# A decoder trunk's MLP on one Trainium2 core: the first matrix by seven half-size products in place of eight

## The chip, the cores and the metric

The kernel runs on one core of a Trainium2 chip. The metric is the device time of one execution in microseconds; the median of several runs is compared. The program is one straight list of instructions for each engine: PE (TensorE, with PEld for its weight loads), DVE (VectorE), ACT (ScalarE), POOL (GpSimd), SP (SyncE, which here issues the weight transfers). An engine works through its list in order, and an instruction waits until semaphores tell it that its inputs are there and its output's buffer is free.

## The reference, cut to what matters

One layer of a decoder for 512 prompt tokens and 8 sample tokens (520 columns in all), width 1024. Token mixing (an RWKV-7 branch beside an RG-LRU branch), cross-attention, and a squared-ReLU MLP of hidden width 4096 follow one another, each with a residual and a layer norm behind it. The edit touches the MLP:

```
D_MODEL = 1024;  D_FF = 4 * D_MODEL;  ALPHA = (2 * DEPTH) ** 0.25
x = LN2(ALPHA * x + cross_attention(x))
h = relu(x @ mlp_up) ** 2          # (520, 1024) @ (1024, 4096)
x = LN3(ALPHA * x + h @ mlp_down)  # (520, 4096) @ (4096, 1024)
```

## The kernel before, in words

Activations lie with features on the 128 partitions and tokens along the free side: `ff0` is x behind the second norm (128 x 8 x 520, eight blocks of 128 features), `q` (also called `z3`) the MLP's sum. Every large product is computed in a number format of the PE that keeps fewer bits than float32, with each operand cut in two: a high part (a copy that rounds) and a low part (what the copy lost). `mm3` then issues three matmuls for each 128 x 128 weight block and each half of the tokens: high weights by high x, high weights by low x, low weights by high x. `Y` is the pair of high and low part of the MLP's input (tiles `hl2`, `hl3`).

`split_w` brings a weight block: a transfer of 512 KB on SP's queue into a raw tile `wr` (three buffers), ACT's copy to the high part `wh` (L95), DVE's subtraction for the low part `wl` (L98).

The MLP runs in NF = 8 groups f of 512 hidden features. A group has four *up units* (`u_up`, 128 hidden columns each, all 8 blocks of K: 8 x 3 x 2 = 48 matmuls of about 260 columns) and, one group later, four *down units* (`u_down`, 256 output columns each as two blocks of K = 512: 2 x 4 x 3 x 2 = 48 matmuls). Behind an up unit come ACT's Relu out of PSUM (L1575), DVE's product max(p,0)*r (L1576), ACT's rounding copy into `hd`, the group's hidden tile (L1577), and DVE's low part of it (L1578). Behind a block of a down unit DVE adds the PSUM result into `q` (L1593, and L1591 for f = 0). `hd` is one of two tiles of the earlier x, called `xH` and `xL` in the rows by turns.

Two helpers order the work. `adv` runs whole units in the order of the list `units`, with the weights of two more units prepared ahead. `halves` runs units by halves of the tokens (`HA` columns first, the rest second), so that the first units of the MLP start while the second norm still works on the other half, and the last four down units finish the first half while the output norm `ln_out` begins. The order in which an engine's instructions stand is set by the program's order and a scheduler behind it, which moves instructions of different units past each other. PSUM has two tiles `mm` of two halves, two tiles `ps`, and one each `ch0` and `ch1`.

Of the kernel before, what the change touches and what calls it, by code (L numbers as in the profile page):

```python
# [36 lines left out]
def build(tc, d, dbg=None):  # L37
# [111 lines left out]
    def unit(src, fn, shape=(KT, 128), extra=0):  # L149
        units.append([src, fn, shape, extra, None])  # L150
# [712 lines left out]
    def slot(t, i, n=1):  # L863
        return t[:, 64 * i:64 * (i + n)].rearrange("p (j b) -> p j b", b=NB)
# [421 lines left out]
    state["x"] = [wx, None]  # L1286
    B1 = ExitStack()
    kv = {}
    at = B1.enter_context(tc.tile_pool(name="at", bufs=2, reuse_waits="tile"))

    def u_rw(i):
        def run(w, half=None):
# [63 lines left out]
    def ln_stats(z, t0, n, wide=False):  # L1356
        if wide:
            p = mmps()
            pp = [p[:, 0], p[:, 1]]
        else:  # L1360
            pp = [ps4(), ps4()]
        st = at.tile([128, 2, 6], F32, tag="bst", name="bst")
# [4 lines left out]
        mv = at.tile([128, 4], F32, tag="mv", name="mv")  # L1367
# [25 lines left out]

    def ln_samples(z):

        zc = at.tile([128, KT, NB], F32, tag="zc", name="zc", bufs=1)
# [16 lines left out]
        t = at.tile([64, 128], F32, tag="sxn", name="sxn", bufs=1)  # L1413
# [155 lines left out]
    def u_up(f, i):  # L1569
        def run(w, half=None):  # L1570
            hd = X[f % 2]
            r = LR.tile([128, T], F32, tag="ya" if i % 2 else "yb", name="r")

            def epi(v, p):
                ACT.activation(v(r), p, AF.Relu)  # L1575
                DVE.scalar_tensor_tensor(v(r), p, 0.0, v(r), op0=OP.max, op1=OP.mult)  # L1576
                ACT.copy(v(hd[:, i, :]), v(r))  # L1577
                DVE.tensor_tensor(v(hd[:, 4 + i, :]), v(r), v(hd[:, i, :].bitcast(F32)), op=OP.subtract)  # L1578
            prod(w, Y, half, epi)
        wunit("mlp_up", f * 512 + i * 128, run, {1: 1, 2: 2, 3: 2}.get(4 * f + i, 0))  # L1580

    def u_down(f, i):
        def run(w, half=None):
            hd = X[f % 2]
            for a in range(2):
                j = 2 * i + a

                def epi(v, p):
                    z = v(z3[:, j, :])
                    if f == 0:  # L1590
                        DVE.scalar_tensor_tensor(z, v(ff0[:, j, :]), ALPHA, p, op0=OP.mult, op1=OP.add)  # L1591
                    else:
                        DVE.tensor_tensor(z, z, p, op=OP.add)  # L1593
                prod(w, (hd[:, 0:4], hd[:, 4:8]), half, epi, [(k, k) for k in range(4)],
                     slice(a * 128, (a + 1) * 128))
        unit(d["mlp_down"][0][f * 512:(f + 1) * 512, i * 256:(i + 1) * 256].rearrange("(k p) n -> p k n", p=128),
             run, (4, 256), int(f == NF - 1 and i == 3))
# [11 lines left out]
    for f in range(NF + 1):
        for i in range(4):  # L1610
            if f < NF:
                u_up(f, i)
        for i in range(4):
            if f > 0:
                u_down(f - 1, i)
# [32 lines left out]
    for h in range(XH):  # L1648
# [10 lines left out]
        if h > 1:  # L1659
# [18 lines left out]
    for n in ("ln3_g", "ln3_b"):  # L1678
# [66 lines left out]
```

## Time and profile before

| | us |
|---|---|
| runs of the kernel before | 1388.75, 1395.51, 1400.05 (median 1395.51) |
| the profiled execution | 1402.65 |
| span of its instructions | 1400.9 |
| PE busy in the span | 1319.4 (94%) |
| DVE busy | 897.1 (64%) |
| ACT busy | 592.1 (42%) |
| POOL busy | 249.7 (18%) |

The profiled execution was 7.1 us above the median of the runs, and within 2.6 us of the slowest. The MLP takes the stretch from about 1006 us (its first half unit) to about 1377 us (the last matmul of its last down unit); the second norm overlaps its begin and the output norm its end.

### The profile page before, as it was taken

How to read it: one execution, taken by the hardware profiler on the slowest of the kernel's cores; microseconds unless marked ns; L12 is line 12 of the kernel's file. 1: busy time of each engine (PE TensorE's matmuls, PEld its weight loads, DVE VectorE, ACT ScalarE, POOL GpSimd, SP SyncE). 2: the span in 40 equal slices, each digit the busy share in tenths (PEclk: the TensorE clock that was granted, in tenths of full speed). 3: DMA queues.
4: the chain of work that ended last, by engine and by line, in shares of the span. 5: the costliest groups of instructions: out<-in, count | busy, mean ns of one | idle time of the engine just before them, and what ended most of it. 6: DMA issues, size and time to landing. Idle time of an engine off the chain costs nothing. (4 is left out here: it accounts for less than half of the span.)

```text
span 1400.9 us, 27360 instructions
## 1 busy us (share of the span) xinstructions
PE 1319.4 (94%) x11242; PEld 1225.5 (87%) x11242; DVE 897.1 (64%) x1742; ACT 592.1 (42%) x1069; POOL 249.7 (18%) x327
## 2 busy tenths in 40 slices
PE   7998999999999998889999999989899999999996
PEld 7997988798878886788879999768899999999996
DVE  5578877796679675887855554756754444444455
ACT  4484375536643665442254334432442332233221
POOL 6311001200020012325423133351110000000002
PEclk9999999998999798898999999999999999999998
DMA  7422412222222032474559545683222233323311
GB/s 197 137 72 63 128 54 63 90 76 65 68 79 84 21 93 91 131 209 138 169 155 288 160 133 176 208 289 121 76 83 86 91 93 92 94 90 97 96 61 62
DMA packets 205971, 160.28 MB, mean 114 GB/s; under 512 B 12430, under 2 KB 190912, under 8 KB 205335
## 3 DMA queue, kind: packets, MB, share of 16 engines
q1 hardware_dynamic: 182502, 104.36, 25.5%
q0 software_dynamic: 14592, 47.80, 10.1%
q10 hardware_dynamic: 8752, 6.39, 1.4%
q8 instruction: 88, 1.44, 0.5%
q14 instruction: 37, 0.30, 0.1%
HBM read 137.11 MB, written 21.40 MB: 113 GB/s over the span
## 5 line engine op out<-in xcount | busy, mean ns | idle before, releaser
L47 PE MATMUL mm<-xH,wh 128*128 128x260 f32 (+2 forms) x1824 | 481.3, 293 | 5.4 <-ACT wh L95 2.2
L47 PE MATMUL mm<-xL,wh 128*128 128x256 f32 (+2 forms) x1824 | 477.2, 290 | 1.3 <-DVE ff L1593 1.0
L47 PE MATMUL mm<-xH,wl 128*128 128x264 f32 (+2 forms) x1568 | 454.8, 290 | 0.8 <-DVE wl L98 0.8
L47 PEld LDWEIGHTS mm<-xH,wh 128*128 128x128 f32 x1824 | 330.9, 191 | 17.0 <-issue 4.3
L95 ACT CAST wh<-wr 128x1024 fp32r<-128x1024 f32 x178 | 185.9, 1050 | 369.9 <-PE mm L47 309.7
L47 PEld LDWEIGHTS mm<-xL,wh 128*128 128x128 f32 x1824 | 330.8, 191 | 9.5 <-issue 5.1
L98 DVE TENSOR_TENSOR wl<-wr,wh 128x1024 fp32r<-128x1024 f32 x178 | 224.0, 1262 | 143.2 <-ACT wh L95 142.5
L47 PEld LDWEIGHTS mm<-xH,wl 128*128 128x128 f32 x1568 | 299.8, 191 | 7.6 <-issue 4.3
L47 PE MATMUL mm<-hl,wh 128*128 128x260 f32 (+2 forms) x1536 | 283.8, 286 | 2.2 <-DVE r L1576 1.4
L47 PEld LDWEIGHTS mm<-hl,wh 128*128 128x128 f32 x1536 | 239.2, 190 | 3.9 <-DVE r L1576 1.6
L47 PE MATMUL mm<-hl,wl 128*128 128x260 f32 (+2 forms) x768 | 219.3, 286 | 0.0
L47 PEld LDWEIGHTS mm<-hl,wl 128*128 128x128 f32 x768 | 145.8, 190 | 0.6 <-issue 0.5
L1593 DVE TENSOR_TENSOR ff<-ff,mm 128x520 f32<-128x520 f32 (+2 forms) x64 | 40.1, 627 | 74.1 <-PE mm L47 73.6
L47 PE MATMUL mm<-xL,wl 128*128 128x260 f32 (+2 forms) x256 | 72.6, 284 | 0.0
L1700 POOL TENSOR_TENSOR xn<-xn,ln_g 128x512 f32<-128x512 f32 x3 | 3.8, 1276 | 355.4 <-ACT xn L1699 355.4
L47 PEld LDWEIGHTS mm<-xL,wl 128*128 128x128 f32 x256 | 48.2, 188 | 0.0
L720 DVE TENSOR_TENSOR Tm<-Tm,tmp 64x30 f32<-64x30 f32 (+14 forms) x120 | 40.5, 337 | 3.4
L47 PE MATMUL mm<-mh,wh 128*128 128x256 f32 x128 | 38.4, 301 | 3.9 <-ACT ft L1129 1.8
L718 DVE TENSOR_TENSOR tmp<-Am,Tm 64x30 f32<-64x30 f32 (+14 forms) x120 | 39.5, 329 | 3.2
L47 PE MATMUL mm<-mh,wl 128*128 128x256 f32 x128 | 37.8, 296 | 3.6 <-DVE wl L98 3.6
L794 DVE SCALAR_TENSOR_TENSOR Sbd<-Sbd,DL,ch 64x64 f32<-64x64 f32 x112 | 31.4, 280 | 15.2 <-PE ch L47 12.4
L533 POOL COPY OUTC<-ut 128x3 f32<-128x3 f32 x8 | 2.9, 366 | 203.0 <-ACT ut L529 203.0
(475 smaller groups left out, 2014.4 us busy)
## 6 DMA issues: line engine op xcount, KB each, us to landing
wr<-in_w_in_dram SPq DMA_DIRECT2D x58, 512.0 KB, 4.4
wr<-in_mlp_up_dram SPq DMA_DIRECT2D x32, 512.0 KB, 4.1
wr<-in_mlp_down_dram SPq DMA_DIRECT2D x32, 512.0 KB, 3.6
vc<-in_cache_mem_v_dram POOLq DMA_DIRECT2D x32, 256.0 KB, 7.3
ff<-in_cache_mem_k_dram POOLq DMA_DIRECT2D x32, 256.0 KB, 4.0
gat_d<-gt POOLq DMA_DIRECT2D x16, 260.0 KB, 2.6
wr<-in_xa_wk_dram SPq DMA_DIRECT2D x8, 512.0 KB, 5.4
wr<-in_xa_wv_dram SPq DMA_DIRECT2D x8, 512.0 KB, 4.9
```

The lines of the kernel that those rows point to most:

```text
L47: r = nc.tensor.matmul(*a, **k)
L95: a = ACT.copy(h, raw)
L98: DVE.tensor_tensor(l, raw, h.bitcast(F32), op=OP.subtract)
L533: POOL.tensor_copy(COUT[:, 0, :, i], ut[:, S:S + 3])
L718: DVE.tensor_tensor(tv, Am[:, i + 1:32, i:i + 1].to_broadcast([64, n, i]), Tm[:, i:i + 1, 0:i].to_broadcast([64, n, i]), op=OP.mult)
L720: DVE.tensor_tensor(Tm[:, i + 1:32, 0:i], Tm[:, i + 1:32, 0:i], tv, op=OP.add)
L794: DVE.scalar_tensor_tensor(Sn[s][hs, hs], So[s][hs, hs], Q[s]["DL"][hs, c - 1:c], PX[hs, cs], op0=OP.mult, op1=OP.add)
L1593: DVE.tensor_tensor(z, z, p, op=OP.add)
L1700: POOL.tensor_tensor(t[0:n], t[0:n], gb[0][0:n, hs], op=OP.mult)
```

## The change

Thirteen pairs of up units, from (1,1) to (7,1) in the changed kernel's naming (group, pair in the group), are no longer computed as 2 x 48 matmuls each. The 1024 x 256 weights of a pair are seen as 2 x 2 blocks (K halves by columns), the 520 tokens as two halves of 260, and the 2 x 2 product is formed from seven half-size products in place of eight (Winograd's form of Strassen's scheme). One product is K = 512, 128 columns, 260 tokens: 4 x 3 = 12 matmuls, so a pair takes 84.

- Four sums of weight blocks (`s1` to `s4`, 128 x 512 each) are formed by POOL for each pair; all seven weight operands are cut into high and low part by ACT and DVE in pieces of 128 x 512 (L1626, L1627), as are the down units' blocks. The cuts run eight blocks ahead (`LEAD`) in a ring of ten slots, and the raw weights have five buffers.
- Four sums of the input (`y_sums`) are formed once, by DVE and POOL, and cut into `TH` and `TL`, each in two pieces of 128 x 520.
- The seven results are combined out of PSUM by ACT (the copy `p1`, L1678) and DVE (seven additions of 128 x 260, L1681 to L1701). Each of the four finished quarters is squared by DVE (L1672), rounded by ACT (L1673), and its low part is formed by POOL (L1674).
- The order of units: six up units (f = 0 and two of f = 1) by halves as before; then the four down units of f = 0; then pair (1,1); then for f = 2 to 7 and each of its two pairs the pair and two down units of f - 1; the last four down units by halves. The input's sums stand beside those first six up units and four down units.
- The norms' small tiles get a pool of their own (`lnp`), the attention's pool `at` goes to the other side of memory and closes earlier, which leaves room for `TH` and `TL`. The third norm's gains and offsets are loaded before the last two down units of f = 6 and no longer before the MLP's full units.

```
     for i in range(6):
         u_up(i // 4, i % 4)
     rest = [u_down(0, i) for i in range(4)] + [u_pair(1, 1)]
     for f in range(2, NF):
         for ip in range(2):
             rest += [u_pair(f, ip), u_down(f - 1, 2 * ip), u_down(f - 1, 2 * ip + 1)]
     last = [u_down(NF - 1, i) for i in range(4)]
...
+    def need(n):
+        while cut[0] < min(n, len(blocks), cap[0]):
+            li, key = blocks[cut[0]]
+            load_to(li + 1)
+            h, l = slot(cut[0])
+            src = got[li][key]
+            ACT.copy(h, src)                                              # L1626
+            DVE.tensor_tensor(l, src, h.bitcast(F32), op=OP.subtract)     # L1627
+            cut[0] += 1
...
+    def mm3b(out, n, x, xk, sl, first=True, last=True):
+        need(n + 1 + LEAD)
+        mm3(out, slot(n), x, [(k, xk + k) for k in range(4)], sl, first, last)
...
+            POOL.tensor_tensor(s1, a21, a22, op=OP.add)                   # L1652
+            POOL.tensor_tensor(s2, s1, a11, op=OP.subtract)
+            POOL.tensor_tensor(s3, a11, a21, op=OP.subtract)
+            POOL.tensor_tensor(s4, a12, s2, op=OP.subtract)               # L1655
...
+            ya, yb = (LR.tile([128, T], F32, tag=tg, name="r").rearrange("p (h n) -> p h n", h=2) for tg in ("ya", "yb"))
+            p1, u2, w5, r = ya[:, 0], ya[:, 1], yb[:, 0], yb[:, 1]
+            def out(v, i, sl):
+                h, l = hd[:, 2 * ip + i, sl], hd[:, 4 + 2 * ip + i, sl]
+                DVE.scalar_tensor_tensor(v, v, 0.0, v, op0=OP.max, op1=OP.mult)   # L1672
+                ACT.copy(h, v)                                                    # L1673
+                POOL.tensor_tensor(l, v, h.bitcast(F32), op=OP.subtract)          # L1674
+            a = t[:, 0, TT]
+            mm3b(a, n0_, Y, 0, T0)
+            ACT.copy(p1, a)                                               # L1678
+            a = t[:, 1, TT]
+            mm3b(a, n0_ + 1, YT[1], 0, TT)
+            DVE.tensor_tensor(u2, a, p1, op=OP.add)                       # L1681
+            a = psc(npair[0] % 2)[:, TT]
+            mm3b(a, n0_ + 2, YT[0], 0, TT)
+            DVE.tensor_tensor(w5, a, u2, op=OP.add)
+            t = mmps()
+            a = t[:, 0, TT]
+            mm3b(a, n0_ + 3, Y, 4, T0)
+            DVE.tensor_tensor(r, a, p1, op=OP.add)                        # L1688
+            out(r, 0, T0)
...
+    def y_sums(z):
...
+        for (lo, hi), a, b in zip(ks, ra, rb):
+            DVE.tensor_tensor(a, z[:, lo, T1], z[:, lo, T0], op=OP.subtract)      # L1722
+            POOL.tensor_tensor(b, z[:, hi, T1], a, op=OP.subtract)                # L1723
...
```

Three places show how the engines' lists change. The first is DVE's list where the MLP's first half units end, from the product of half unit (5,0) (the sixth unit's first half) to that of (3,1). `r` is the square's tile, `xH`/`xL` the hidden tile's low part, `ts` a sum of the input, `TL` its low part, `wl` the low part of weights. Before:

```order
L1576 SCALAR_TENSOR_TENSOR r<-mm,r 128x256
L1578 TENSOR_TENSOR xL<-r,xL 128x256
L1576 SCALAR_TENSOR_TENSOR r<-mm,r 128x264
L1578 TENSOR_TENSOR xH<-r,xH 128x264
L1576 SCALAR_TENSOR_TENSOR r<-mm,r 128x264
L1578 TENSOR_TENSOR xL<-r,xL 128x264
L1576 SCALAR_TENSOR_TENSOR r<-mm,r 128x264
L1578 TENSOR_TENSOR xL<-r,xL 128x264
L98 TENSOR_TENSOR wl<-wr,wh 128x1024
L1576 SCALAR_TENSOR_TENSOR r<-mm,r 128x264
```

In the changed kernel the same stretch of DVE's list, from the product of (0,1) on, reads (twelve rows, which reach only to that of (2,1)):

```order
L1577 SCALAR_TENSOR_TENSOR r<-mm,r 128x264
L1627 TENSOR_TENSOR wl<-wr,wh 128x512 x2
L1579 TENSOR_TENSOR xH<-r,xH 128x264
L1719 TENSOR_TENSOR TL<-ts,TH 128x520
L1577 SCALAR_TENSOR_TENSOR r<-mm,r 128x264
L1719 TENSOR_TENSOR TL<-ts,TH 128x520
L1627 TENSOR_TENSOR wl<-wr,wh 128x512
L1579 TENSOR_TENSOR xH<-r,xH 128x264
L1627 TENSOR_TENSOR wl<-wr,wh 128x512
L1719 TENSOR_TENSOR TL<-ts,TH 128x520
L1577 SCALAR_TENSOR_TENSOR r<-mm,r 128x264
L1627 TENSOR_TENSOR wl<-wr,wh 128x512
```

Between the products of two half units, where one low part stood alone, there are now three to five more instructions: pieces of the input's sums and half blocks of weights.

The second place is POOL's list. Before, POOL had nothing between the second norm's last low part and the output norm. In the changed kernel stand there, around pair (1,1), the sums for pair (2,1), the four low parts of pair (1,1), the four of pair (2,0), and the sums for pair (3,0):

```order
L1652 TENSOR_TENSOR ws<-wr 128x512
L1654 TENSOR_TENSOR ws<-wr 128x512
L1653 TENSOR_TENSOR ws<-ws,wr 128x512
L1655 TENSOR_TENSOR ws<-wr,ws 128x512
L1674 TENSOR_TENSOR xL<-r,xL 128x260 x4
L1674 TENSOR_TENSOR xH<-r,xH 128x260 x4
L1652 TENSOR_TENSOR ws<-wr 128x512
L1654 TENSOR_TENSOR ws<-wr 128x512
L1653 TENSOR_TENSOR ws<-ws,wr 128x512
L1655 TENSOR_TENSOR ws<-wr,ws 128x512
L1674 TENSOR_TENSOR xH<-r,xH 128x260 x4
```

The sums of a pair that comes later stand ahead of the low parts of the pair that is running; pairs (1,1) and (2,0) have no down unit between them.

The third place is DVE's list in the steady stretch, one pair's seven results with the cuts between them (`ps`, `ch`, `mm` are PSUM tiles, `ws` a weight sum). In the changed kernel:

```order
L1681 TENSOR_TENSOR r<-mm,r 128x260
L1684 TENSOR_TENSOR r<-ch,r 128x260
L1627 TENSOR_TENSOR wl<-wr,wh 128x512
L1627 TENSOR_TENSOR wl<-ws,wh 128x512
L1688 TENSOR_TENSOR r<-mm,r 128x260
L1627 TENSOR_TENSOR wl<-ws,wh 128x512
L1672 SCALAR_TENSOR_TENSOR r<-r 128x260
L1692 TENSOR_TENSOR r<-ps,r 128x260
L1693 TENSOR_TENSOR r<-ps,r 128x260
L1672 SCALAR_TENSOR_TENSOR r<-r 128x260
L1627 TENSOR_TENSOR wl<-wr,wh 128x512
L1697 TENSOR_TENSOR r<-mm,r 128x260
```

Before, two up units had there:

```order
L1576 SCALAR_TENSOR_TENSOR r<-mm,r 128x520
L1578 TENSOR_TENSOR xH<-r,xH 128x520
L98 TENSOR_TENSOR wl<-wr,wh 128x1024
L1576 SCALAR_TENSOR_TENSOR r<-mm,r 128x520
L1578 TENSOR_TENSOR xH<-r,xH 128x520
L98 TENSOR_TENSOR wl<-wr,wh 128x1024
```

Four long instructions for the two units' results became eleven short ones that each wait for one of the seven products or for the one ahead, and the weights are cut in smaller pieces between them.

More of the change, by code (lines that the diff above doesn't have):

```diff
@@ L1361, in ln_stats @@
             pp = [ps4(), ps4()]
[L1362 removed]
+        st = lnp.tile([128, 2, 6], F32, tag="bst", name="bst")
         for h in range(2):
@@ L1580, in u_up, with slot @@
         wunit("mlp_up", f * 512 + i * 128, run, {1: 1, 2: 2, 3: 2}.get(4 * f + i, 0))
-    def u_down(f, i):
-        def run(w, half=None):
+    LEAD = 8
+    ring, loads, got, blocks = [], [], [], []
+    cut, cap = [0], [8]
+    def slot(n):
+        if n // 2 == len(ring) < 5:
+            p = (wsp, wx, state["x"][1], wsp, wsp)[n // 2]
+            ring.append((p.tile([128, KT, 128], F32R, tag="wh", name="wh"),
+                         p.tile([128, KT, 128], F32R, tag="wl", name="wl")))
+        t, k = ring[n // 2 % 5], n % 2 * 4
+        return t[0][:, k:k + 4], t[1][:, k:k + 4]
@@ new lines, in build, with raw_tile, more_raws @@
+    spare = []
+    def raw_tile(src, shape):
+        raws.append(raws.pop(0))
+        raw = raws[-1]
+        if raw in spare:
+            if shape[0] == 4:
+                raw = raw.rearrange("p (k a) n -> p k (a n)", a=2)
+        else:
+            raw = raw.tile([128, *shape], F32, tag="wr", name="wr")
+        SP.dma_start(out=raw, in_=src)
+        return raw
+    def more_raws():
+        for tg in ("wh", "wl"):
+            spare.append(state["x"][1].tile([128, KT, 128], F32, tag=tg, name="wr"))
+        raws.extend(spare)
@@ new lines, in load_to @@
+    def load_to(n):
+        while len(got) < min(n, len(loads)):
+            got.append(loads[len(got)]())
+    def need(n):
[7 more added lines that the diff above has]
+            cut[0] += 1
+            if cut[0] < len(blocks) and blocks[cut[0]][0] > li:
+                got[li] = None
+                load_to(li + 4 if cap[0] > 8 else min(li + 4, 4))
@@ new lines, in build, with cut_ @@
+    YT = []
+    def y_sums(z):
+        TH = tp.tile([128, 4, 4, HT], F32R, name="TH")
+        TL = tp.tile([128, 4, 4, HT], F32R, name="TL")
+        YT[:] = [(TH[:, i], TL[:, i]) for i in range(4)]
+        ks = [(slice(k, k + 2), slice(4 + k, 6 + k)) for k in (0, 2)]
+        ra, rb = ([LR.tile([128, T], F32, tag=tg, name="ts").rearrange("p (k n) -> p k n", k=2) for tg in tags]
+                  for tags in (("tr", "a0"), ("ti", "xc")))
+        def cut_(i, r):
+            for (lo, hi), e in zip(ks, r):
+                ACT.copy(TH[:, i, lo], e)
+                DVE.tensor_tensor(TL[:, i, lo], e, TH[:, i, lo].bitcast(F32), op=OP.subtract)
+        for (lo, hi), a, b in zip(ks, ra, rb):
+            DVE.tensor_tensor(a, z[:, lo, T1], z[:, lo, T0], op=OP.subtract)
+            POOL.tensor_tensor(b, z[:, hi, T1], a, op=OP.subtract)
+        yield
+        cut_(0, ra)
+        yield
+        cut_(1, rb)
+        for (lo, hi), a, b in zip(ks, ra, rb):
+            POOL.tensor_tensor(b, z[:, hi, T0], b, op=OP.subtract)
+            DVE.tensor_tensor(a, z[:, hi, T1], z[:, lo, T1], op=OP.subtract)
+        yield
+        cut_(2, ra)
+        cut_(3, rb)
+        yield
@@ L1584, in run, with load @@
+    def u_down(f, i):
+        n0_ = len(blocks)
+        def load():
+            w = raw_tile(d["mlp_down"][0][f * 512:(f + 1) * 512, i * 256:(i + 1) * 256].rearrange(
+                "(k p) n -> p k n", p=128), (4, 256))
+            return {a: w[:, :, a * 128:(a + 1) * 128] for a in range(2)}
+        loads.append(load)
+        for a in range(2):
+            blocks.append((len(loads) - 1, a))
+        def run(half=None):
             hd = X[f % 2]
@@ L1593, in epi @@
                         DVE.tensor_tensor(z, z, p, op=OP.add)
[L1594 to L1597, printed above, removed]
+                need(n0_ + a + 1 + LEAD)
+                prod(slot(n0_ + a), (hd[:, 0:4], hd[:, 4:8]), half, epi, [(k, k) for k in range(4)])
+        return run
     for i in range(KT):
@@ L1608, in build @@
         u_wo(i)
[L1609 to L1615, printed above, removed]
+    for i in range(6):
+        u_up(i // 4, i % 4)
+    rest = [u_down(0, i) for i in range(4)] + [u_pair(1, 1)]
+    for f in range(2, NF):
+        for ip in range(2):
+            rest += [u_pair(f, ip), u_down(f - 1, 2 * ip), u_down(f - 1, 2 * ip + 1)]
+    last = [u_down(NF - 1, i) for i in range(4)]
     def norm(z, gn, bn, name):
@@ L1663, in build, with values_end @@
     ln, sm = norm(ff0, "ln2_g", "ln2_b", "LN2")
-    halves(4, *hs(0, 0, 1, 2, 3), lambda: sample_values(XH - 1), 6, *hs(1, 0, 1), 8, *hs(0, 4, 5, 6, 7), ln[0],
+    def values_end():
+        sample_values(XH - 1)
+        B1.close()
+    halves(4, *hs(0, 0, 1, 2, 3), values_end, 6, *hs(1, 0, 1), 8, *hs(0, 4, 5, 6, 7), ln[0],
            *hs(1, 2, 3), 9, (4, 1), 10, (5, 1), 11, (6, 1), 12, (7, 1), 13, ln[1])
-    halves((0, 0), 6, (1, 0), sm, (2, 0), sm, (3, 0), sm, (4, 0), sm, (5, 0), (0, 1), (4, 1), (5, 1), 7, (1, 1), 8, (2, 1), 9, (3, 1))
-    x.close()
-    B1.close()
+    Tx = ExitStack()
+    tp = Tx.enter_context(tc.tile_pool(name="tp", bufs=1, reuse_waits="tile"))
+    ysg = y_sums(ff0)
+    ys = lambda: next(ysg, None)
+    nd = lambda n: lambda: need(n)
+    halves((0, 0), 6, (1, 0), sm, (2, 0), sm, (3, 0), sm, (4, 0), sm, (5, 0), (0, 1), nd(2), (1, 1), nd(4), (2, 1),
+           nd(5), (3, 1), more_raws, nd(6), ys, (4, 1), nd(7), ys, (5, 1), nd(8), ys)
+    for n, u in enumerate(rest[:4]):
+        u()
+        if n == 0:
+            ys()
+            load_to(5)
+        elif n == 1:
+            cap[0] = len(blocks)
+    for u in rest[4:-2]:
+        u()
+    Tx.close()
     C_ = ExitStack()
@@ L1682, in build @@
         gs.append(t)
-    adv(len(units) - 4 - state["run"])
+    for u in rest[-2:]:
+        u()
     def ln_out(half):
@@ L1707, in ln_out @@
                 (SP if h else ACT).dma_start(out=d["y_prompt"][0, t0:t0 + n, hs], in_=t[0:n])
-    halves(*hs(0, 0, 1, 2, 3), lambda: ln_out(0), *hs(1, 0, 1, 2, 3), lambda: ln_out(1))
+    for half in range(2):
+        for u in last:
+            u(half)
+        ln_out(half)
     C_.close()
+    x.close()
     B.close()
```

47 lines of the change are left out of this document (41 added, 6 removed).

## The prediction

> **What bounds the kernel now.** I read the page's busy line and its forty slices first, then the granted clock and busy times of stretches of the MLP, then the engines' groups there, then single rows at its begin.
>
> ```profile
> PE   7998999999999998889999999989899999999996
> DVE  5578877796679675887855554756754444444455
> POOL 6311001200020012325423133351110000000002
> ```
>
> In the last ten slices (35 us each) PE stands at 9 with DVE at 4 and POOL at 0: that is the MLP. The next view gives busy time and instruction counts for whole stretches: two groups of 384 matmuls, then all full units and the last ones' first part.
>
> ```profile
> core 0: us, PE busy (x) PEld busy (x) DVE busy (x) ACT busy (x) POOL busy (x), PEclk, DMA share, GB/s
> 1062.31:1108.61 46.30, 46.20 (x384) 46.02 (x385) 20.52 (x25) 12.92 (x17) 0.00 (x0) 1.00 0.30 92
> 1293.84:1340.14 46.30, 46.20 (x384) 46.02 (x385) 20.52 (x25) 12.91 (x17) 0.00 (x0) 1.00 0.31 92
> 1031.00:1372.00 341.00, 340.27 (x2830) 338.99 (x2829) 151.88 (x187) 95.14 (x123) 0.00 (x0) 1.00 0.29 87
> ```
>
> PE is busy 340.27 of 341 us at a granted clock of 1.00; DVE has 45% of the time, ACT 28%, POOL none. So the stage is bound by the number of matmuls alone, and each costs 46.30/384 = **0.1206 us**. Whatever takes matmuls away is paid in full, as long as PE does not begin to wait.
>
> **What goes.** Thirteen pairs take 84 in place of 96 matmuls: 156 fewer. The columns stay 260, the partitions 128, so the price stays: 156 x 0.1206 = **18.8 us**. What is left to work out is how much PE waits in the new arrangement, because the work that was hidden grows and the buffers shrink.
>
> **The steady stretch: a pair and two down units.** PE: 180 matmuls x 0.1206 = 21.7 us (84 of them, 10.1 us, in the pair). DVE's durations come from these groups (mean ns of one behind the comma):
>
> ```profile
> L98 DVE TENSOR_TENSOR wl<-wr,wh 128x1024 fp32r<-128x1024 f32 x61 | 75.5, 1240 | 92.6 <-ACT wh L95 92.6
> L1563 DVE TENSOR_TENSOR xL<-ch,xH 128x512 fp32r<-128x512 f32 x8 | 5.5, 686 | 0.5 <-ACT xH L1562 0.5
> L1593 DVE TENSOR_TENSOR ff<-ff,mm 128x520 f32<-128x520 f32 x48 | 33.4, 696 | 62.1 <-PE mm L47 61.6
> L1593 DVE TENSOR_TENSOR ff<-ff,mm 128x264 f32<-128x264 f32 x8 | 3.4, 424 | 5.5 <-PE mm L47 5.5
> L1576 DVE SCALAR_TENSOR_TENSOR r<-mm,r 128x264 f32<-128x264 f32 x6 | 2.6, 428 | 4.1 <-ACT r L1575 4.1
> L1700 POOL TENSOR_TENSOR xn<-xn,ln_g 128x512 f32<-128x512 f32 x3 | 3.8, 1276 | 355.4 <-ACT xn L1699 355.4
> L1690 POOL TENSOR_TENSOR sxn<-sxn,ln_bs 64x128 f32<-64x128 f32 x1 | 0.4, 446 | 0.1
> ```
>
> Eleven cuts of 128 x 512 at 0.69 are 7.6 us (two halves at 0.69 for one whole at 1.24: the finer pieces cost a little), seven additions at 0.42 are 2.9, four squares at 0.43 are 1.7, four down additions at 0.70 are 2.8: **15.1 us of DVE beside 21.7 of PE**, 70% where it was 45%. POOL has four sums at 1.28 and four low parts; for 128 x 260 no row stands, and the line through 0.446 (128 elements) and 1.276 (512) gives an estimate of 0.73, so 5.1 + 2.9 = 8.0 us. Each engine by itself has room. They do not run by themselves, though. DVE's rows while POOL works on the norm, and then undisturbed:
>
> ```profile
> 992.05 3.89 DVE L98 TENSOR_TENSOR wl<-wr,wh 128x1024 fp32r<-128x1024 f32 x2 [0.58 <-ACT wh L95]
> 999.00 1.22 DVE L98 TENSOR_TENSOR wl<-wr,wh 128x1024 fp32r<-128x1024 f32 x1 [0.44 <-ACT wh L95]
> 1012.77 0.42 DVE L1578 TENSOR_TENSOR xH<-r,xH 128x256 fp32r<-128x256 f32 x1
> 1016.53 6.16 POOL L1438 TENSOR_TENSOR hl<-ff,hl 128x512 fp32r<-128x512 f32 x4 [21.67 <-ACT hl L1437]
> 1016.78 2.12 DVE L98 TENSOR_TENSOR wl<-wr,wh 128x1024 fp32r<-128x1024 f32 x1
> 1018.82 0.53 DVE L1436 TENSOR_SCALAR ff<-ps,PT 128x256 f32<-128x256 f32 x1
> 1019.28 0.41 DVE L1576 SCALAR_TENSOR_TENSOR r<-mm,r 128x256 f32<-128x256 f32 x1
> 1020.28 1.27 DVE L1578 TENSOR_TENSOR xH<-r,xH 128x256 fp32r<-128x256 f32 x1
> ```
>
> Beside POOL's four operations from 1016.53 on, a cut takes 2.12 in place of 1.22 and a low part 1.27 in place of 0.42: an operation with two inputs in SBUF loses about 0.9 us each time it meets one of POOL's. Operations that read PSUM (0.53, 0.41) lose nothing. In a steady period the cuts and squares are open to this, the additions are not. Eight meetings at 0.9 for 1.28-us operations, less for the short ones, are some 5 us: DVE at 20 of 21.7 us, still below PE. The ends of this term: no meeting costs DVE 15.1; if DVE stands still for all of POOL's time, 15.1 + 8.0 = 23.1 us, and DVE is the bound by 1.4 us a period.
>
> The Trainium skill, page "SBUF — State Buffer", section "Who interferes with whom", speaks against the change here: a DVE instruction with two SBUF inputs and a GpSimd instruction that reads SBUF exclude each other for the whole instruction, and one with at most one SBUF input is free of it. The rows above agree in kind (0.9 us against nothing); with every POOL operation charged whole, the rule's sum is the 23.1 us.
>
> **Inside a pair.** The second product to be combined can't start freely: `p1` (ACT, L1678) must leave the PSUM tile `mm` before the product that uses its other half may write there. PE's list puts 8 matmuls of another product in between, 8 x 0.12 = 0.96 us. ACT's list has a cut ahead of the copy:
>
> ```profile
> L1577 ACT CAST xL<-r 128x520 fp32r<-128x520 f32 x14 | 8.8, 627 | 19.6 <-DVE r L1576 19.6
> L1575 ACT ACTIVATE r<-mm 128x264 f32<-128x264 f32 x6 | 2.4, 392 | 6.0 <-PE mm L47 6.0
> ```
>
> A cut of 0.63 that begins about when the product's last matmuls do, then a copy of about 0.39, ends 1.1 us behind the product, with handing over: 0.15 us late. The next close place is the addition `r` (L1688), for which PE has 12 matmuls (1.45 us) of cover, while DVE may hold a cut (0.69) and a POOL meeting (0.9) ahead of it. I take 0.17 us a pair, **2 us** in twelve pairs; the ends are 0 and 0.5 us a pair (6 us).
>
> **The begin (the six units by halves).** Before, each half unit takes PE 24 matmuls, 2.9 us, and DVE mostly waits:
>
> ```profile
> 1029.07 0.22 DVE L1450 TENSOR_TENSOR hl<-ff,hl 128x64 fp32r<-128x64 f32 x1
> ...
> 1033.83 0.43 DVE L1576 SCALAR_TENSOR_TENSOR r<-mm,r 128x264 f32<-128x264 f32 x1 [1.03 <-ACT r L1575]
> 1036.67 0.43 DVE L1576 SCALAR_TENSOR_TENSOR r<-mm,r 128x264 f32<-128x264 f32 x1 [1.50 <-ACT r L1575]
> ...
> 1042.58 0.43 DVE L1576 SCALAR_TENSOR_TENSOR r<-mm,r 128x264 f32<-128x264 f32 x1
> 1045.58 0.42 DVE L1576 SCALAR_TENSOR_TENSOR r<-mm,r 128x264 f32<-128x264 f32 x1
> ```
>
> Each product `r` frees the PSUM tile that the half unit after next writes. In the changed list, from the first of the input's sums to the product of (3,1), DVE has eighteen operations of 128 x 512 or 128 x 520 (eight of them ahead of the product of (0,1)) and ten of the small ones: 18 x 0.695 + 10 x 0.43 = **16.8 us of work**. The sums need the norm's last output, whose low part ends at 1029.3 (first row). The product of (3,1) must be there when half unit (5,1) starts, 0.7 us before the product of (4,1) at 1045.58 (last row): 15.6 us. So DVE is late by 1.2 us by its work alone. On top come POOL's four operations of `y_sums`, which read SBUF and meet DVE's sums and cuts: 4 x 0.9 = 3.6. I take **4.8 us**. The least is 0.5 (a part of the sums done while DVE waits anyway), the most 8 (every cut also waits for ACT's high part, and ACT has eight more at 0.63 there). Behind (5,1) the four down units, 5.8 us of PE each, ask little of DVE, and what is then left is caught up.
>
> **The seam of pairs (1,1) and (2,0).** No down unit lies between them. POOL's list has the sums for pair (2,1) ahead of the low parts of pair (1,1), and these sums wait for raw weights, whose transfer SP issues only when DVE has cut an earlier block, about where the first product of (1,1) ends. The low parts free the tile `ya` that the copy `p1` of (2,0) writes.
>
> ```profile
> wr<-in_mlp_up_dram SPq DMA_DIRECT2D x26, 512.0 KB, 4.1
> ```
>
> From the end of that first product POOL is done after 4.1 (landing) + 5.1 (four sums) + 2.9 (four low parts) + about 1 (the issue and handing over) = 13.1 us, up to 17 with DVE in the way. PE reaches the product that needs the tile after 72 matmuls of (1,1), 12 of the first product and 12 that stand ahead, 96 x 0.12 = 11.6 us. Late by 1.5 to 5.5; I take **4 us** (nearer the upper end, since the cuts of pair (2,0) run beside POOL there). Later pairs have 11.6 us of down units in between: the same queue is hidden.
>
> **What costs nothing.** SP issues 14 more transfers, each of 512 KB, in a stage where the transfers take 30% of the queues; the time of SP is free. Half of the raw tiles now wait for four sums, but five tiles stand in place of three. The third norm's parameters come some 320 us later, still a dozen us ahead of their use; if they were late, they would cost up to the 5 us of a landing. The end (last down units by halves and the output norm) keeps its order.
>
> **Sum.** 18.8 - 4.8 - 4 - 2 = **8.0 us** gained. On the profiled execution: 1402.65 - 8.0 = 1394.7. That execution lay 7.1 us above the median of the runs, in parts that the edit does not touch as far as I can see; on the median: 1395.5 - 8.0 = **1387.5 us**.
>
> **Rivals.**
>
> *The stalls are small (0.28).* If POOL lands between DVE's long operations and the seam is covered, 2 us are lost in all: 1395.5 - 16.8 = 1378.7. For it speaks that every engine is below 95% in the steady sum; against it the two sums above, each of which is late before any contention.
>
> *DVE becomes the bound in every period (0.14).* With the 23.1 us, 12 x 1.4 = 16.8 is lost beside the 8.8 at begin and seam: 18.8 - 16.8 - 8.8 = -6.8, so 1402.3. For it: the rows with 0.9 us lost to one meeting. Against it: half of DVE's work in the down units meets no POOL operation if the sums come in one run.
>
> *Slower: the loss falls inside the pair (0.10).* DVE's list in a pair has seven cuts less what the down units carry, the additions and the squares, about 9.5 us beside 10.1 of PE. Four sums that meet cuts there (3.6) make it 13.1, and since the additions stand behind the cuts in the list, PE waits out the difference in each of 13 pairs, with the lead of eight blocks no help: about 2.5 us x 13 = 32 in place of my 2, 1395.5 - 18.8 + 8.8 + 32 = 1417.5. It decides from 0.8 us a pair (no gain) and 1.9 a pair (slower by 1%). Against it: the sums wait for a landing, and that comes with most sums in the down units.
>
> *The matmuls cost the same time in fewer numbers (0.03):* if weight loads set the pace and the smaller products loaded more slowly, the time would stay at 1395. The loads are as many as the matmuls, 46.02 of 46.30 us, and fall with them.
>
> **How the numbers follow.** The forecast has 0.45, with its own range of 1381 to 1393. The range reaches from 1375 (the first rival with nothing lost, and 2 us for the runs' own spread) to 1403 (DVE as the bound); the slower rival's upper part and a little of each end are left out. A measurement of this kernel tells about 1% (14 us) from no change: faster than 1381.5 holds the first rival but for a little, and a tenth of the forecast's case, 0.32; slower than 1409.5 holds the slower rival and a little of DVE as the bound, 0.11; 0.57 remains between.
>
> **What would show it.** 180 matmuls in 21.7 us and PE busy above 99% in a late period: the steady sum is right. PE waits of about 5 us in all for DVE's product (L1577) between 1030 and 1050, and one wait of about 4 us for ACT's copy (L1678) near 1085: the two stalls. POOL at some 37% and DVE at 70% to 90% in the stage. The prediction is wrong if PE waits in every pair by over half a microsecond, or not at all at the seam.

## The result, and the profile after

| | before | changed |
|---|---|---|
| median of 20 runs each | 1394.99 us (1387.51 to 1406.24) | 1387.76 us (1382.13 to 1396.75) |
| ratio to before | | 0.9946, 95% interval 0.9924 to 0.9968 |
| profiled execution, span | 1400.9 us | 1380.4 us |

The change makes the kernel 0.5% faster, some 7.5 us (4 to 11 by the interval). The two profiled spans differ by 20.5 us, which must not be taken for the effect. The first place to read lies ahead of everything that the edit touches: one matmul of the second norm's stretch, before and after (start, duration, instruction, and in brackets the idle time ahead of it):

```profile
996.34 0.39 PE L47 MATMUL mm<-xH,wh 128*128 128x264 f32 x1 [0.42 <-DVE ff L1345]
```

```profile
984.42 0.39 PE L47 MATMUL mm<-xH,wh 128*128 128x264 f32 x1 [0.42 <-DVE ff L1346]
```

11.9 us of the 20.5 had come about by then, in a part in which both programs issue the same work: that is the spread between executions. (In the eleven profiles of the changed kernel and of its variants below, whose edits all lie behind it, the same matmul stands anywhere from 984.4 to 996.8 us.) So the change is read from one stage: from the wait of 1.40 us at the third half unit, which both kernels have, to the last wait of 0.97 us ahead of the output norm. Before:

```profile
1019.74 0.51 PE L47 MATMUL mm<-hl,wh 128*128 128x256 f32 x2 [1.40 <-DVE r L1576]
1377.67 0.51 PE L47 MATMUL mm<-xL,wh 128*128 128x264 f32 x2 [0.97 <-DVE ff L1593]
```

After, with those waits in between that are new and reach half a microsecond:

```profile
1002.86 0.51 PE L47 MATMUL mm<-hl,wh 128*128 128x256 f32 x2 [1.40 <-DVE r L1577]
1018.43 0.40 PE L47 MATMUL mm<-hl,wh 128*128 128x264 f32 x1 [0.56 <-DVE r L1577]
1023.63 0.51 PE L47 MATMUL mm<-hl,wh 128*128 128x264 f32 x2 [2.02 <-DVE r L1577]
1043.76 0.51 PE L47 MATMUL mm<-xH,wh 128*128 128x260 f32 x2 [2.48 <-DVE ff L1756]
1079.48 0.58 PE L47 MATMUL mm<-TH,wh 128*128 128x260 f32 x1 [4.74 <-ACT r L1678]
1357.14 0.39 PE L47 MATMUL mm<-xL,wh 128*128 128x264 f32 x1 [0.97 <-DVE ff L1758]
```

The stage takes 357.9 us before and 354.3 after. All new waits lie in its first 80 us: 2.6 us at the half units, 2.5 at the first down unit, 4.7 at the seam of pairs (1,1) and (2,0), 9.8 in all. Behind the last of them no wait reaches a quarter of a microsecond until the end. The steady stretch, two periods of a pair and two down units each (columns as in the prediction's stretches), which did the work of one group of 46.30 us before, and the time right behind the seam:

```profile
1101.46:1145.04 43.58, 43.58 (x363) 43.24 (x362) 32.26 (x53) 16.73 (x32) 19.51 (x16) 1.00 0.32 99
1232.31:1275.95 43.64, 43.64 (x363) 43.29 (x361) 32.10 (x53) 16.74 (x32) 19.36 (x16) 1.00 0.33 97
1079.48:1083.60 4.12, 4.12 (x19) 4.12 (x20) 1.70 (x4) 1.09 (x2) 0.00 (x0) 0.50 0.44 128
```

A period of 180 matmuls is 21.8 us (the counts of two periods pass 360, since they take in matmuls that began just ahead of the window). PE shows as full, DVE stands at 74% and POOL at 45%: each pair gains (46.30 - 43.6) / 2 = 1.35 us, 13 pairs 17.5 us. The last row shows what the prediction did not have: behind the seam's wait the granted clock is 0.50 for 4.1 us, 19 matmuls take 4.12 us in place of 2.3, and 1.8 us more are lost.

PE is not quite as full as the busy column says, since a matmul's end is modelled and a short delay disappears in it. The starts show one in every pair, at the second product, which needs the PSUM tile that ACT's copy L1678 leaves:

```profile
1101.59 0.62 ACT L1626 CAST wh<-wr 128x512 fp32r<-128x512 f32 x1 [0.87 <-PE mm L47]
1102.12 0.37 ACT L1678 COPY r<-mm 128x260 f32<-128x260 f32 x1
1102.30 0.28 PE L47 MATMUL ch<-TL,wh 128*128 128x260 f32 x1
1102.54 0.39 PE L47 MATMUL mm<-TH,wh 128*128 128x260 f32 x1
1102.77 0.28 PE L47 MATMUL mm<-TL,wh 128*128 128x260 f32 x1
```

Three starts that should lie 0.12 us apart lie 0.24 and 0.23 apart, just behind the end of the copy at 1102.49: 0.23 us lost. The same stands at the same place in twelve of the thirteen pairs (all but the one at the seam), 0.22 to 0.24 each, 2.7 us in all. The 1.35 us a pair have this taken off already.

So the trace's account is 17.5 - 9.8 - 1.8 = 5.9 us gained. The stage shows 3.6, mostly because another low spell of the clock (1005 to 1009 us, some 1.7 us lost, behind the norm's waits) fell inside it after; before, the like lay ahead of it. The other 0.6 us are open.

The stage leaves something out, though. From the matmul of the first place (996.34 and 984.42) to the stage's start pass 23.4 us before and 18.4 after, so from that matmul on the two profiles differ by 8.6 us. Before, PE waits there for an addition of the second norm that stands in DVE's list behind a cut, and the cut for a weight block that landed late; after, the same wait is shorter:

```profile
1002.69 1.04 ACT L95 CAST wh<-wr 128x1024 fp32r<-128x1024 f32 x1 [3.72 <-DMA wr<-in_mlp_up_dram]
1005.39 0.69 PE L52 MATMUL ps<-ident,ff 128*128 128x128 f32 x2 [3.87 <-DVE ff L1346]
```

```profile
990.78 0.44 PE L52 MATMUL ps<-ident,ff 128*128 128x128 f32 x2 [1.18 <-DVE ff L1347]
```

Of the 5.0 us, 2.7 are this wait, and the rest goes with the low spell that lay there before (1004.0 to 1010.9 us). In all eleven profiles of changed kernels the wait is 1.2 to 2.0 us and the stretch 18.4 to 20.7. SP issues the transfers at the same distance from that matmul in both kernels. Of the kernel before there is one profile, so it is not shown whether the longer wait belongs to that kernel or to that execution.

### The profile page after: what moved, and what is told of

The parts are those of the page before. It is cut to its first block, busy times and chain, and to the rows that moved or that the text cites. A ratio compares the mean times of both kernels' runs of the same rounds, so it can differ in the third digit from the quotient of the medians.

```text
span 1380.4 us, 27562 instructions
## 1 busy us (share of the span) xinstructions
PE 1294.0 (94%) x11086; PEld 1199.2 (87%) x11086; DVE 986.4 (71%) x1942; ACT 622.2 (45%) x1187; POOL 378.6 (27%) x435
## 3 DMA queue, kind: packets, MB, share of 16 engines
q8 instruction: 87, 1.43, 0.4%
## 5 line engine op out<-in xcount | busy, mean ns | idle before, releaser
L95 ACT CAST wh<-wr 128x1024 fp32r<-128x1024 f32 x120 | 125.0, 1049 | 176.8 <-PE mm L47 128.5
L47 PE MATMUL mm<-hl,wh 128*128 128x260 f32 (+2 forms) x1016 | 193.1, 288 | 4.8 <-DVE r L1577 4.0
L98 DVE TENSOR_TENSOR wl<-wr,wh 128x1024 fp32r<-128x1024 f32 x120 | 152.8, 1279 | 52.2 <-ACT wh L95 51.5
L47 PEld LDWEIGHTS mm<-hl,wh 128*128 128x128 f32 x1016 | 160.0, 192 | 6.9 <-DVE r L1577 4.6
L47 PE MATMUL mm<-hl,wl 128*128 128x260 f32 (+2 forms) x508 | 146.5, 288 | 0.0
L1626 ACT CAST wh<-wr 128x512 fp32r<-128x512 f32 x103 | 63.6, 620 | 121.5 <-PE mm L47 89.6
L1627 DVE TENSOR_TENSOR wl<-wr,wh 128x512 fp32r<-128x512 f32 x103 | 92.5, 900 | 12.8 <-ACT wh L1626 12.8
L47 PEld LDWEIGHTS mm<-hl,wl 128*128 128x128 f32 x508 | 97.3, 192 | 0.6 <-issue 0.5
L1674 POOL TENSOR_TENSOR xL<-r,xL 128x260 fp32r<-128x260 f32 x28 | 26.3, 947 | 79.6 <-ACT xL L1673 79.6
L1626 ACT CAST wh<-ws 128x512 fp32r<-128x512 f32 x52 | 32.1, 620 | 33.4 <-PE mm L47 22.1
L1627 DVE TENSOR_TENSOR wl<-ws,wh 128x512 fp32r<-128x512 f32 x52 | 38.3, 739 | 6.2 <-ACT wh L1626 4.4
```

The lines of the kernel that those rows point to most:

```text
L47: r = nc.tensor.matmul(*a, **k)
L95: a = ACT.copy(h, raw)
L98: DVE.tensor_tensor(l, raw, h.bitcast(F32), op=OP.subtract)
L1626: ACT.copy(h, src)
L1627: DVE.tensor_tensor(l, src, h.bitcast(F32), op=OP.subtract)
L1674: POOL.tensor_tensor(l, v, h.bitcast(F32), op=OP.subtract)
```

## The experiments

All are the changed kernel with one edit or two. For each stands the length of the same stage in its own profile (357.9 before, 354.3 changed), and where it was timed the ratio to before, beside 0.9946 for the change. New waits of PE are given as half units / first down units / seam; the change has 2.6 / 2.5 / 4.7. The 1.4 us that were there before are left out.

### One down unit between the pairs

```
-    rest = [u_down(0, i) for i in range(4)] + [u_pair(1, 1)]
+    rest = [u_down(0, 0), u_down(0, 1), u_down(0, 2), u_pair(1, 1), u_down(0, 3)]
-    cut, cap = [0], [8]
+    cut, cap = [0], [6]
-                load_to(li + 4 if cap[0] > 8 else min(li + 4, 4))
+                load_to(li + 4 if cap[0] > 6 else min(li + 4, 4))
```

> One down unit of group 0 is put between pairs (1,1) and (2,0), so the seam gets 5.8 us more of PE work; the scheduler then also puts the input's sums behind the six units by halves. Theory (the seam's wait of 4.74 us comes from POOL's sums for pair (2,1) and the low parts behind them, and costs the clock as well: 0.50 of full speed for some 4.5 us behind it, worth 2.3 us): no wait on the copy p1 at pair (2,0), no clock below 1.00 there, 7 us gained against the changed kernel, more if the waits of 0.6 and 2.0 us at the half units go with the moved sums. Rival (the idle time alone counts, the low clock comes from elsewhere): 4.7 us gained and the clock still drops near there.

Stage 349.9 us, 1378.95 us, ratio 0.9854 (0.9803 to 0.9904). Waits 0 / 3.8 / 0.6. The waits of PE in that stage (total, times, longest):

```profile
PE mm L47 <- DVE ff L1756: 3.8, 3, 1.8
PE mm L47 <- DVE r L1577: 1.4, 1, 1.4
PE mm L47 <- ACT r L1678: 0.6, 1, 0.6
```

The seam falls from 4.7 to 0.6, and no low clock follows it (one follows the wait of 1.8 us at the down units, from 1065.0 us on). The moved sums of the input took their delay along, though: the half units no longer wait, and the down units behind them wait 3.8 us. Two places had changed at once, hence the seventh experiment.

### Earlier raw tiles for the first pair

```
-    (0, 1), nd(2), (1, 1), nd(4), (2, 1), nd(5), (3, 1), more_raws, nd(6), ys, ...
+    (2, 1), (3, 1), more_raws, (0, 1), nd(2), (1, 1), nd(4), nd(5), nd(6), ys, ...
```

> Only the order of the second halves of the first units is changed: (2,1) and (3,1) go ahead of (0,1) and (1,1), so two raw tiles come free two half units (5.8 us) earlier and the transfers of pair (1,1)'s weights start earlier. Theory (the wait of 2.5 us at the first down unit comes from ACT's list, where a cut of a weight sum stands ahead of the last half unit's rounding copy and waits for sums whose raw weights land late): that wait goes, 2.6 us gained in the trace; the seam keeps its 4.7 us. Rival (DVE is simply behind from the input's sums): the wait stays above 1.5 us.

Stage 353.4, 1387.09 us, ratio 0.9926 (0.9890 to 0.9961). The wait on the first down unit's addition (L1756) is gone, the seam has its 4.7:

```profile
PE mm L47 <- DVE r L1577: 4.8, 5, 1.8
PE mm L47 <- ACT r L1678: 4.7, 1, 4.7
```

The cause is the one named. In the change, POOL's sum waits for raw weights, ACT's cut for a sum, and the last half unit's copy stands behind that cut:

```profile
1037.07 1.29 POOL L1652 TENSOR_TENSOR ws<-wr 128x512 f32<-128x512 f32 x1 [14.39 <-DMA wr<-in_mlp_up_dram]
...
1040.89 0.62 ACT L1626 CAST wh<-ws 128x512 fp32r<-128x512 f32 x1 [4.53 <-POOL ws L1653]
1041.41 0.41 ACT L1578 CAST xL<-r 128x264 fp32r<-128x264 f32 x1
```

But little came of it: of 4.8 us, 1.4 were there before, and 3.4 are new, where the change had 2.6 here and 2.5 there: 0.7 of them stand where the first down unit begins, now for DVE's product (L1577). The wait moved to DVE's next late place, and the gain of 1 us in the stage can't be told from none in the times.

### The low parts on DVE

```
-                POOL.tensor_tensor(l, v, h.bitcast(F32), op=OP.subtract)
+                DVE.tensor_tensor(l, v, h.bitcast(F32), op=OP.subtract)
```

> The four low parts of each pair are formed by DVE in place of POOL; everything else as in the change. Theory of the prediction (the seam is late since the low parts stand behind four sums in POOL's list): the wait at pair (2,0) falls from 4.7 us to 1 us or less. Rival (DVE is late there, its cuts and squares losing time to the sums that run beside them, so that the last quarter is squared late): 3 us or more stay. In the steady pairs DVE goes from about 72% to 80% with PE still not waiting, by both.

Waits 2.5 / 1.6 / 2.9 (stage 355.0 with three low spells of the clock in it, one run 1388.97 us). The seam falls by 1.9 us only, so neither theory holds alone. POOL's list in the change, around the seam, shows both:

```profile
1068.16 1.59 POOL L1652 TENSOR_TENSOR ws<-wr 128x512 f32<-128x512 f32 x1 [15.58 <-DMA wr<-in_mlp_up_dram]
1069.71 1.48 POOL L1654 TENSOR_TENSOR ws<-wr 128x512 f32<-128x512 f32 x1
1071.15 1.48 POOL L1653 TENSOR_TENSOR ws<-ws,wr 128x512 f32<-128x512 f32 x1
1072.71 1.62 POOL L1655 TENSOR_TENSOR ws<-wr,ws 128x512 f32<-128x512 f32 x1
1074.30 3.19 POOL L1674 TENSOR_TENSOR xL<-r,xL 128x260 fp32r<-128x260 f32 x3
1078.29 0.73 POOL L1674 TENSOR_TENSOR xL<-r,xL 128x260 fp32r<-128x260 f32 x1 [0.80 <-ACT xL L1673]
```

The sums wait for the raw weights, three low parts stand behind them as foreseen, but the fourth waits for ACT, and so for DVE. DVE in the same microseconds:

```profile
1068.51 1.52 DVE L1672 SCALAR_TENSOR_TENSOR r<-r 128x260 f32<-128x260 f32 x1
1069.96 0.42 DVE L1692 TENSOR_TENSOR r<-ps,r 128x260 f32<-128x260 f32 x1
1071.40 1.78 DVE L1627 TENSOR_TENSOR wl<-wr,wh 128x512 fp32r<-128x512 f32 x1
1073.44 1.44 DVE L1627 TENSOR_TENSOR wl<-wr,wh 128x512 fp32r<-128x512 f32 x1
1074.81 0.95 DVE L1672 SCALAR_TENSOR_TENSOR r<-r 128x260 f32<-128x260 f32 x1
1076.82 0.95 DVE L1672 SCALAR_TENSOR_TENSOR r<-r 128x260 f32<-128x260 f32 x1
```

A square of 0.43 takes 0.95 to 1.52, a cut of 0.69 up to 1.78, while the addition from PSUM keeps its 0.42. So POOL holds the pair's tile up in two ways, by its own queue and by slowing DVE. How much is each is not shown: the 1.9 us are the least that the queue costs, since this version also gives DVE four more operations a pair, and no run leaves the weight sums out at the seam.

In the steady pairs the expectation missed. Two periods of this version:

```profile
1108.20:1151.80 43.60, 43.60 (x363) 43.27 (x362) 30.70 (x61) 16.72 (x32) 11.06 (x8) 1.00 0.32 96
```

DVE forms eight low parts more than in the change, some 3 us of work, and is yet busy 1.5 us less (30.7 for 32.2): 70%, not 80%. By this sum, an estimate, each low part on POOL cost DVE 0.5 to 0.6 us, more than the 0.42 us that DVE takes to form it itself.

### Eight products again

```
             mm3b(a, n0_ + 6, YT[3], 0, TT)
+            mm3b(a, n0_ + 6, YT[3], 0, TT)
```

> The seventh product of each pair is computed twice into the same tile, so a pair has 96 matmuls again and all else stays as in the change. Theory (each matmul costs 0.1206 us and nothing else sets the pace): a steady period grows from 21.6 to 23.0 us, 18.8 us in all less some 1.5 us of the seam's wait: the profiled stage is about 17 us longer than the change's, and the kernel slower than before by 10 us. Rival (weight loads, DVE or POOL share in setting the pace): the period grows by less than 1 us.

Stage 370.9, 1407.96 us in one run; waits 2.5 / 2.2 / 3.4. Two periods:

```profile
1111.39:1157.83 46.44, 46.44 (x387) 46.10 (x385) 32.20 (x53) 16.92 (x32) 18.71 (x16) 1.00 0.30 91
```

A period is 23.2 us, 1.43 more than in the change: 12 matmuls at 0.119. The price of a product is the predicted one, and the steady pace goes by the number of matmuls; the 0.23 us behind the copy L1678 stand in these pairs as well. The experiment also shows what the rearrangement costs by itself: with 96 matmuls a pair the stage is 13 us longer than before, so the saved product carries the gain, and the rest is loss.

### No POOL in the input's sums

```
-            POOL.tensor_tensor(b, z[:, hi, T1], a, op=OP.subtract)
...
-            POOL.tensor_tensor(b, z[:, hi, T0], b, op=OP.subtract)
-        cut_(1, rb)
+        cut_(1, ra)
...
-        cut_(3, rb)
+        cut_(3, ra)
```

> POOL's four operations of the input's sums are left out, so two of the four sums are copies of the other two (this part of the result is left out); DVE's and ACT's work is the same as in the change. Theory (in the half units DVE is late by the 16.8 us of its own work and by four meetings with POOL, 0.9 us each): the waits for DVE's product, 0.6 and 2.0 us in the change beside the 1.4 that was there before, fall to 1.2 us or less together, and DVE's pieces of the sums all take about 0.7 us. Rival (DVE's work alone makes it late, POOL costs nothing): 2 us or more stay.

Stage 350.6, one run 1390.95 us; waits 0 / 1.7 / 4.7. The pieces of the sums on DVE, first in the change and then here (count, total, mean ns):

```profile
L1719 DVE TENSOR_TENSOR TL<-ts,TH 128x520 fp32r<-128x520 f32 x8 | 7.5, 949 | 0.0
L1722 DVE TENSOR_TENSOR ts<-ff 128x520 f32<-128x520 f32 x2 | 2.5, 1255 | 0.0
L1730 DVE TENSOR_TENSOR ts<-ff 128x520 f32<-128x520 f32 x2 | 2.4, 1231 | 0.0
```

```profile
L1719 DVE TENSOR_TENSOR TL<-ts,TH 128x520 fp32r<-128x520 f32 x8 | 5.5, 693 | 0.0
L1722 DVE TENSOR_TENSOR ts<-ff 128x520 f32<-128x520 f32 x2 | 1.4, 694 | 0.0
L1729 DVE TENSOR_TENSOR ts<-ff 128x520 f32<-128x520 f32 x2 | 1.3, 692 | 0.0
```

12.4 us against 8.2: the four meetings cost 4.2 us, 1.05 each, and without them DVE's work makes nobody wait. The half units' wait is POOL's doing. (Two of the four input sums are missing here, so this version serves for its times alone.)

### The weight sums twice

```
             POOL.tensor_tensor(s4, a12, s2, op=OP.subtract)
+            POOL.tensor_tensor(s3, a11, a21, op=OP.subtract)
+            POOL.tensor_tensor(s1, a21, a22, op=OP.add)
+            POOL.tensor_tensor(s2, s1, a11, op=OP.subtract)
+            POOL.tensor_tensor(s4, a12, s2, op=OP.subtract)
```

> POOL forms the four weight sums of each pair twice, 5.1 us more POOL work in each period; nothing else changes. Theory (DVE has some 6 us of slack in a period of 21.6 us, and a meeting with POOL costs it 0.3 to 0.9 us): PE still does not wait in the steady pairs, the period stays at 21.6 us; only the seam grows, from 4.7 to 9 us or more. Rival (the port that DVE and POOL share bounds the stage): the period grows by 1.4 us or more, 17 us in all.

Stage 365.4, one run 1399.08 us; waits 2.5 / 6.5 / 9.4. Two late periods:

```profile
1120.00:1163.60 43.60, 43.60 (x363) 43.27 (x362) 35.22 (x53) 16.73 (x32) 31.89 (x25) 1.00 0.33 98
```

POOL goes from 19.5 to 31.9 us, DVE from 32.3 to 35.2, and PE is as full as before. 12.4 us of POOL work cost DVE 3 us, a quarter of it. The steady pairs have room to spare; the begin has none, and takes 4.0 and 4.7 us of the added 5.1 at its two places.

### The down unit between, the sums early

```
-    rest = [u_down(0, i) for i in range(4)] + [u_pair(1, 1)]
+    rest = [u_down(0, 0), u_down(0, 1), u_down(0, 2), u_pair(1, 1), u_down(0, 3)]
-    cut, cap = [0], [8]
+    cut, cap = [0], [6]
-                load_to(li + 4 if cap[0] > 8 else min(li + 4, 4))
+                load_to(li + 4 if cap[0] > 6 else min(li + 4, 3))
```

> As the first experiment (one down unit between pairs (1,1) and (2,0)), but the weights of pair (1,1) are loaded after the input's sums, which keeps these at the half units as in the change. Theory: the seam's wait of 4.7 us goes as it did there; the waits of 0.6 and 2.0 us at the half units come back; the wait at the first down unit is 2.5 us as in the change or longer, since the pair stands a down unit earlier. Rival (the first experiment gained by the sums' new place alone): the seam still waits 2 us or more.

Stage 347.4, one run 1378.81 us. The waits:

```profile
PE mm L47 <- DVE r L1577: 4.1, 4, 2.0
PE mm L47 <- DVE ff L1756: 1.0, 2, 0.5
PE mm L47 <- ACT r L1678: 0.6, 1, 0.6
```

The seam is gone with the sums where they were, so the first experiment's gain there was the down unit's. The first down unit's wait fell too, from 2.5 to 0.5 (another 0.5 stands where the pair behind the moved down unit begins), which no theory had; with one unit fewer to load ahead of it the first pair's weights came sooner, and POOL's first weight sum begins 28.1 us behind the stage's start in place of 34.2. Timed in a series of its own:

> The kernel of the seventh experiment again, timed: one down unit between pairs (1,1) and (2,0), the rest as in the change. By the trace of the seventh experiment the stage is 6.8 us shorter than the change's and 10.5 us shorter than before: 0.990 to 0.992 of the time before where the change had 0.9946. Rival (the gain in one profile was the clock's luck): 0.994 or more.

1383.88 us in 12 runs, ratio 0.9917 (0.9883 to 0.9952), as expected; the stage is 347.5. The interval overlaps the change's, so in times alone the step from 0.9946 is not shown; the traces show 6.8 us less in the stage, and both times the same waits. Of the 6.8, 5.6 are waits; the rest goes with the clock, since one low spell of 3.4 us falls in this stage and two, 10.2 us together, in the change's.

### With the early raw tiles

> The down unit between the pairs, the input's sums at the half units, and the early raw tiles of the second experiment together. Theory: no seam, no wait at the first down unit, some 3.5 us of waits at the half units as in the second experiment; against the change 7 us less for the seam and its clock, and 1 to 2 us for the rest: 1379 us where the change has 1388. Rival (the early gains are each given back as the next wait): not below 1384.

Both edits (this one and the earlier raw tiles) give a stage of 347.8, 1384.23 us, ratio 0.9897 (0.9840 to 0.9955). Half units 2.6, down units 3.0 (2.0 of it for DVE's product of the last half units), seam 0.6. The raw tiles make it worse: the waits are 6.1 us in all where the seventh experiment has 4.2, and the stage is as short only since no low spell of the clock fell in it, against one there. The rival's bound of 1384 and the theory's 1379 both lie within the spread of four runs.

### The input's sums wholly on DVE

```
-            POOL.tensor_tensor(b, z[:, hi, T1], a, op=OP.subtract)
+            DVE.tensor_tensor(b, z[:, hi, T1], a, op=OP.subtract)
...
-            POOL.tensor_tensor(b, z[:, hi, T0], b, op=OP.subtract)
+            DVE.tensor_tensor(b, z[:, hi, T0], b, op=OP.subtract)
```

> The down unit between the pairs (sums early, as in the seventh experiment), and the four operations that POOL does in the input's sums are done by DVE. Theory (at the half units the meetings with POOL make DVE late, not the amount of its work; the fifth experiment had no wait there with 16.8 us of DVE work): DVE has 2.8 us more work and about 4 us less of meetings, the waits of 0.6 and 2.0 us go, 1 us or less of new waits stays in the half units, and about 1379 us or less where the change has 1388. Rival (DVE has no room left at the half units): 3 us or more of waits there, as in the seventh experiment.

On top of the seventh experiment's edit. Stage 346.7, 1378.24 us, ratio 0.9890 (0.9842 to 0.9937), and the waits:

```profile
PE mm L47 <- DVE r L1577: 3.6, 2, 2.2
PE mm L47 <- ACT r L1678: 0.6, 1, 0.6
```

No wait is left between half units, though DVE has more to do. But one of 2.2 us stands now where the first down unit begins, more than the 1 us expected: there the weight sums of the first pair meet DVE. This version and the first experiment's have the lowest times of all; 0.9890 and 0.9854 with their intervals don't tell which is better, and both lie below the kernel before by 1% to 1.5%.

## Why the prediction was right, point by point

The time (1387.5 forecast, 1387.8 measured), the sign and the size came out, but the terms of the sum less well than the sum:

- **156 matmuls at 0.1206, 18.8 us**: 17.5 by the periods. A product costs 1.43 us, as good as forecast (fourth experiment). The difference is in the mean of a matmul, 21.8/180 = 0.1211 where the group before had 0.1206, and the starts settle it: between delays matmuls follow each other every 0.1197 us before (381 from 1062.62 us on) and every 0.1199 after (178 from 1102.77 us on). What lifts the mean is, before, some 0.3 us lost where each group begins and, after, the 0.23 us behind the copy L1678 in each pair. The 17.5 thus have the loss inside the pairs (below) in them already.
- **Steady stretch, PE stays the bound**: right, PE waits for nothing in eleven pairs but the copy L1678. DVE was put at 20 of 21.7 us and is at 16.1; POOL has 9.8 in place of 8.0. A meeting costs DVE less than 0.9 here: 0.5 to 0.6 us for a low part (third experiment) and 0.4 for a weight sum (sixth: 3 us for eight). The rival by which DVE becomes the bound is out, by the doubled sums too. The Trainium skill's exclusive lock (page "SBUF — State Buffer", section "Who interferes with whom") agrees in kind with the squares of 0.95 and 1.52 us and with additions from PSUM that stay at 0.42, but charging each POOL operation whole, as the rule's sum in the prediction did, is too much for a list in which half of the time DVE works from PSUM or waits: the two figures above make some 4 us a period, an estimate, where POOL is busy 9.8.
- **2 us inside the pairs**: 2.7. This step was right in place, cause and nearly in size: the copy L1678 stands behind a cut in ACT's list and ends too late, and 0.17 us a pair were forecast where 0.23 are lost in each of twelve. The busy column hides it. The second close place, the addition L1688, makes nobody wait.
- **4.8 us at the half units**: 2.6. The price of a meeting was right (1.05 us for 0.9), the place too. The term of DVE's own lateness (1.2 us) was not there at all: without POOL nothing waits, and of the four meetings' 4.2 us DVE had room for 1.6.
- **Four down units "ask little of DVE, and what is then left is caught up"**: this step failed. 2.5 us were lost there, since ACT's list had cuts of weight sums ahead of the last half unit's copy, and POOL got the raw weights only at 1037.07 us.
- **4 us at the seam**: 4.7, at the place and for the wait named. Of the cause, the queue behind the sums is at least 1.9 us by the third experiment. That the rest is DVE, slowed by the same sums, is what the rows suggest; no run separates the two.
- **Not in the sum**: the low clock, 1.8 us behind the seam; the delay at the begin of each group before, which the change takes away (some 2 us in all, already in the 17.5); and the wait ahead of the MLP, 2.7 us shorter in the profile after, which may be no part of the effect.

By the trace the account is 5.9 us in the MLP, or 8.6 with the wait ahead of it, where 8.0 were forecast and 7.5 (4 to 11) measured: the exactness of the total is luck, its terms missed by up to 2.5 us with both signs.

## What to carry to other kernels

A change that takes work from a full engine gains in the steady stretch and loses at the seams: look at the first pass through a new pipeline, where transfers, sums and cuts have no work ahead to hide behind, and put independent work between two units that hand over one buffer. An engine with much idle time isn't free if its operations slow down a neighbour at the moment when that neighbour is waited for: POOL's operations made PE wait nowhere in the steady pairs and 2.6 us at the begin, and a low part of 0.42 us given to POOL cost DVE more than to form it itself. Where a busy column says that an engine is full, look at the starts: 2.7 us were lost here in pieces of 0.23 that no idle time shows. And compare profiles of two kernels over the stage that changed, between two instructions that both have, since the spans here differed by 11.9 us before that stage began; then look at the stretch just ahead of it too, which held another 5 us.

## What the runs showed of the hardware beyond that

PE's granted clock falls to 0.50 during a wait of PE or up to 1.4 us behind it. In the stretch from 984 to 1110 us of the twelve profiles there are 23 such low spells, and each lasts 3.4, 6.8 or 10.2 us: once, twice or three times 3.41. In the changed kernel they run from 1005.3 to 1008.8 and from 1077.0 to 1083.9 us, the second with its first 2.5 us inside the seam's wait; the longest, 10.2 us, belongs to the wait of 9.4 us with the sums formed twice.

In all six kernels with the seam's wait (2.9 to 9.4 us) such a spell came with it; in the four without it (0.6 us left; five profiles), none stood there. Waits of about 2 us were followed by one in some profiles (fourth experiment: behind 2.2 us at the first down unit; first: behind 1.8) and not in others (none behind the 2.02 and 2.48 us of the changed kernel). A wait of this size can therefore cost PE more than its length, by 1.8 us at the seam; that the wait causes the spell is what the order in time and the four kernels without both suggest, and what decides in the cases near 2 us is open.
